# Convolution taps weighed on ScalarE and added in pairs on VectorE, with a higher background rate, in a two-layer conditioned trunk

## The chip, the core and the metric

The kernel runs on one core of a Trainium2 chip. The metric is the device time in microseconds (us) of one execution. TensorE (PE) multiplies matrices, with its weight loads shown as PEld; VectorE (DVE), ScalarE (ACT) and GpSimd (POOL) do the elementwise work; SyncE (SP) issues the DMA transfers of the weights. Each engine works through its own list of instructions in a fixed order, and engines wait for each other through semaphores.

## The reference

Two layers over 256 tokens of 2048 channels, in float32. The first layer mixes tokens with a 31-tap depthwise causal convolution on 1024 channels beside a gated chunk mixer on the other 1024; the second with causal pooling. Each layer then has a dense SwiGLU. Every sub-layer is scaled, shifted and gated by vectors that are computed from a conditioning vector `c`.

```python
def reference(x, c, ...):
    cond = silu(c)
    for l in range(2):
        sh1, sc1, g1, sh2, sc2, g2 = split(cond @ ada_w[l] + ada_b[l], 6)
        h = rmsnorm(x, norm_mix_g[l]) * (1 + sc1) + sh1
        y = mixer_ab(h, ...) if l == 0 else mixer_c(h, ...)
        x = x + g1 * y
        h = rmsnorm(x, norm_ffn_g[l]) * (1 + sc2) + sh2
        x = x + g2 * ((silu(h @ ffn_w1[l]) * (h @ ffn_w3[l])) @ ffn_w2[l])
    return rmsnorm(x, final_g)

def mixer_ab(h, ...):
    a_val, a_gate, b_u, b_v = split(h @ w_in, 4)          # 1024 columns each
    a = a_val * sigmoid(a_gate)
    a = causal_depthwise_conv(a, conv_w) + conv_b          # 31 taps per channel
    a = silu(layernorm(a, a_g, a_b))
    b = b_u * chunk_mix(layernorm(b_v))
    return concat(a, b) @ w_out
```

## The kernel before

**Splits and units.** Every weight comes from memory as a `raw` tile of 128x1024 float32 (12 buffers), on SP's queue. `split` turns it into two parts of a lower precision: `hi` by a cast on ACT (L164), and `lo`, the rest, by a subtraction on DVE (L165); there are four buffers of each. PE multiplies the activations with them (L213 and L214 with `hi`, L219 with `lo`): twelve matmuls of 128x512 for one split. A `unit` is two splits, 24 matmuls. `chain` runs the units of one result, and the 128x512 results lie in PSUM tiles called `mm`.

**Work beside the units.** Two mechanisms put other work between the units.

- `tick`, called after every unit, adds `rate` to a credit and runs one step of the background list `bg` for each whole credit. In the first mixer (`mixer_ab`) the list holds 56 steps: the gate `g1` (16 steps, sums on PE at L312), four quarters of the second scale `SC2` (5 steps each, on PE at L378, then a column step at L405 to L415) and four quarters of the second shift `SH2` (5 steps each). A quarter of the shift is summed on DVE: each of its first four steps has four instructions on `accq` (L383, L385, 128x512) and two weight loads, and its fifth turns the sum into columns on PE (`ps_col`, L405) and adds the bias (L411). `RATES[0]` is the rate of this stage, which has 36 units. What is left in the list by its end is run in `started`, at the beginning of the first SwiGLU: there `between` runs the steps of a quarter beside the units of the quarter ahead of it, and `close` finishes it.
- `split` calls `filler` `FILL` times, and each call runs the generators in `fill` up to their next `yield`. There are three: `conv(0)`, `conv(4)` and `norm_a`.

**The convolution.** `aT` holds the gated values with channels on partitions, eight tiles of 128 channels, and `co` the running sum. `conv` goes through the 31 taps for two channel tiles at a time: L670 for the first tap, with the bias, then L675, which multiplies a shifted window of `aT` by one weight per partition and adds it to `co`, 128x256, on DVE. There is a `yield` after each of the 248 instructions. `norm_a` is the layer norm over channels that follows: column sums on PE (`ps_ln`, L685), mean on ACT, subtraction on DVE (L690), squares on ACT (`sq`), sums on PE (`ps_var`, L698), a power on POOL, a copy on DVE (`rw`), a transposed spread on PE (`ps_rstd`, L711), a product on DVE (L713), SiLU on ACT (L716), and the split into `mh` (ACT, L488) and `ml` (DVE, L489), which are the left operands of the last matmuls.

**Order in the mixer.** The fillers start after the first unit of `proj(DH + 512)`. Then come the other three units of it, eight units for `v`, eight for `u` and eight for `out_half(1)`, the half of the output projection that takes the gated chunk mixer: 27 units. Whatever is then left in `fill` is run at once, and `out_half(0)`, eight units, multiplies the convolution's result. After every two units of an output half, `residual` multiplies by the gate (`gy`, L598) and adds to `x` (L599) on DVE, for both blocks of 128 tokens. At the end, `x` is normalized (`xr`, L476), transposed, scaled and split for the first SwiGLU.

The order on each engine is settled before the run by the framework in which the kernel is written, from the order of the calls and from priorities (`soon` raises one); it can differ from the order of the code.

Of the kernel before, what the change touches and what calls it, by code (L numbers as in the profile page):

```python
# [8 lines left out]
F32 = mybir.dt.float32  # L9
F32R = mybir.dt.float32r  # L10
AF = mybir.ActivationFunctionType
ALU = mybir.AluOpType
PSUM = bass.MemoryType.PSUM

P = 128
D = 2048
KT = D // P
T = 256
# [6 lines left out]
PADC = 16  # L25
EPS = 1e-6
RAW, HL = 12, 4
RATES = 1.28, 0.71, 0.5, 1.0, 1.0
PE2 = False
PE3 = True  # L30
FILL = 5
SOON = 100
WINDOWS = (2, 4, 8, 16)
SH1, SC1, G1, SH2, SC2, G2 = range(6)
# [2 lines left out]
class Trunk:  # L37
# [122 lines left out]
    def split(self, raw):  # L160
# [4 lines left out]
        nc.vector.tensor_tensor(lo, raw, hi.bitcast(F32), op=ALU.subtract)  # L165
        for _ in range(FILL):
            self.filler()
# [436 lines left out]
    def mixer_ab(self, e, nxt):  # L604
        nc, i = self.nc, self.i
        with ExitStack() as s:
            p = s.enter_context(self.tc.tile_pool(name="ab", bufs=1))
            aT = p.tile([P, HT, PADA + T], F32, name="aT")
            nc.gpsimd.memset(aT[:, :, :PADA], 0.0)
            wcT = p.tile([P, HT, P], F32, name="wcT")  # L610
            cw = p.tile([P, HT, 32], F32, name="cw")
# [33 lines left out]
            for b in range(NB):  # L645
                e.start(b)
                for q in range(4):
                    e.prep(b, q)
            held = self.started(e, [(w_in, 0), (w_in, DH), (w_in, 512)], RATES[0], params)
            act = e.act  # L650

            co = p.tile([P, HT, T], F32, name="co", tag="co")
# [9 lines left out]
            done = []  # L662

            def conv(k0):
                for t0 in (k0, k0 + 2):
                    for j in range(CW):
                        for k in (t0, t0 + 1):
                            src = aT[:, k, j : j + T]
                            if j == 0:
                                nc.vector.tensor_scalar(  # L670
                                    co[:, k, :], src, cw[:, k, 0:1], self.col("conv_b", k),
                                    op0=ALU.mult, op1=ALU.add,
                                )
                            else:
                                nc.vector.scalar_tensor_tensor(  # L675
                                    co[:, k, :], src, cw[:, k, j : j + 1], co[:, k, :],
                                    op0=ALU.mult, op1=ALU.add,
                                )
                            yield

            def norm_a():
# [61 lines left out]

            gated(0, held[0], held[1])
            self.late.append(lambda: self.fill.append(conv(0)))
            gated(1, held[2], proj(DH + 512))
            self.late.append(lambda: self.fill.extend([conv(4), norm_a()]))


# [126 lines left out]
    def ffn(self, p, l, e, nxt, gen_g2, rest):  # L876
# [6 lines left out]
        if e.parts:  # L883
            for q in range(1, 4):
                e.prep(0, q)
            for q in range(4):
                e.prep(1, q)
            ps = self.started(e, [(w1, 0), (w3, 0), (w1, 512)], RATES[1])
            held = {(1, 0): ps[0], (3, 0): ps[1], (1, 1): ps[2]}
        else:  # L890
            ps = self.begun(e, [(w1, 0), (w3, 0), (w1, 512)], rest)
            self.rate = RATES[2]
            held = {(1, 0): ps[0], (3, 0): ps[1], (1, 1): ps[2]}
# [72 lines left out]
    def run(self):  # L966
# [32 lines left out]
        with ExitStack() as s:  # L999
# [9 lines left out]
            self.finish(more)  # L1009
            self.rate = RATES[3]  # L1010
            rest = self.add(
                self.mod_cols(1, SC2, 3, PE3, ffn1.gs, "ffn_g"), self.mod_cols(1, SH2, 3, PE3, ffn1.sh)
            )
            self.mixer_c(mix1, ffn1)
            self.rate = RATES[4]
            self.g2 = self.gate()
# [59 lines left out]
```

## Time and profile before

| | |
|---|---|
| median of 3 runs | 2015.34 us (2014.14 to 2020.6) |
| profiled execution, its time | 2013.25 us |
| its span, first to last instruction | 2011.5 us |
| mean clock granted to TensorE | 0.98 |
| first mixer after its first four results begin (started) | about 165 to 429 us |
| change-over to the first SwiGLU | 429 to 443 us |
| start of the first SwiGLU (`started`) | 443 to about 515 us |

Times in the profile are counted from the first instruction. In a row of the timeline the first two numbers are start and duration in us, `xN` means that N instructions were merged in the row, and the bracket gives how long the engine was idle before it and what it waited for. Instructions of one engine overlap a little, so that the distance between two starts is shorter than a duration; sums go by the distance.

### The profile page before, as it was taken

Reading aid. Unit: us, or ns where it says so; the run is one execution under the profiler, and the core shown is the slowest. Engines: PE = TensorE matmul, PEld = TensorE weight load, DVE = VectorE, ACT = ScalarE, POOL = GpSimd, SP = SyncE. Lnnn points to the kernel's source line nnn. Section 1 sums busy time; section 2 is a strip of 40 time slices with the busy share of each in tenths; the row PEclk is TensorE's granted clock in tenths of the full one; section 3 lists DMA queues with packets and bytes.
Section 4 is the critical chain, followed back from the end, with each engine's and each line's share of the span. In section 5 each row is a group of like instructions: output and inputs, shape, how many; then the busy total and the mean of one; then the engine's idle time right before and its main releaser. Section 6 shows DMA issues by size and latency. Waiting matters only on the chain.

```text
span 2011.5 us, 24248 instructions
## 1 busy us (share of the span) xinstructions
PE 1947.4 (97%) x8864; PEld 1541.1 (77%) x8864; DVE 1431.0 (71%) x1724; ACT 839.6 (42%) x1021; POOL 34.7 (2%) x91
## 2 busy tenths in 40 slices
PE   4989999998999999999999999999999999999998
PEld 2557677777887888887878887888788888888886
DVE  4767999798878878777887788867555444554455
ACT  3234343454444344443344346544434444334443
POOL 1000000000000000000120000000000000000000
PEclk7889999989999999999999999999999999999999
DMA  8997988789888899988988887989666666566651
GB/s 337 347 366 258 341 275 291 271 264 350 301 278 321 320 337 328 311 288 317 335 316 296 283 288 263 338 272 319 198 188 189 190 192 191 180 191 193 191 186 46
DMA packets 250344, 540.39 MB, mean 269 GB/s; under 512 B 16521, under 2 KB 17849, under 8 KB 249840
## 3 DMA queue, kind: packets, MB, share of 16 engines
q1 hardware_dynamic: 248472, 536.99, 78.4%
q10 hardware_dynamic: 1752, 1.86, 0.3%
q8 instruction: 69, 1.13, 0.2%
q14 instruction: 51, 0.42, 0.1%
HBM read 536.68 MB, written 2.10 MB: 268 GB/s over the span
## 4 chain that ended last, share of the span: by engine, by line
PE 94%; DVE 2%; DMA 2%; ACT 1%; issue 1%; POOL 0%; SPq 0%; POOLq 0%; DVEq 0%; ACTq 0%
PE mm L213 28%; PE mm L214 27%; PE mm L219 27%; PE ps_ada L378 2%; PE ps_col L405 2%; DVE accq L385 1%; PE mt L213 1%; PE mt L214 1%; PE mt L219 1%; PE tp L590 1%; PE ps_ada L312 1%; PE tp L479 1%; DMA prm<-in_a_conv_w_dram 1%; PE tp L837 1%; DMA raw<-in_pool_w_dram 0%
## 5 line engine op out<-in xcount | busy, mean ns | idle before, releaser
L164 ACT CAST hi<-raw 128x1024 fp32r<-128x1024 f32 x632 | 665.3, 1054 | 974.2 <-PE mm L214 898.8
L165 DVE TENSOR_TENSOR lo<-raw,hi 128x1024 fp32r<-128x1024 f32 x632 | 770.6, 1223 | 419.1 <-ACT hi L164 410.4
L213 PE MATMUL mm<-hi,ah 128*128 128x512 f32 x1568 | 618.4, 395 | 2.9 <-ACT ah L488 2.9
L214 PE MATMUL mm<-hi,al 128*128 128x512 f32 x1568 | 612.2, 391 | 0.0
L219 PE MATMUL mm<-lo,ah 128*128 128x512 f32 x1568 | 421.9, 390 | 0.0
L213 PEld LDWEIGHTS mm<-hi,ah 128*128 128x128 f32 x1568 | 295.6, 189 | 91.8 <-issue 14.3
L214 PEld LDWEIGHTS mm<-hi,al 128*128 128x128 f32 x1568 | 295.5, 188 | 61.5 <-issue 0.8
L219 PEld LDWEIGHTS mm<-lo,ah 128*128 128x128 f32 x1568 | 294.4, 188 | 61.2
L213 PE MATMUL mm<-hi,hh 128*128 128x512 f32 x704 | 280.4, 398 | 0.0
L214 PE MATMUL mm<-hi,hl 128*128 128x512 f32 x704 | 277.3, 394 | 0.0
L350 DVE SCALAR_TENSOR_TENSOR acc<-raw,cond,acc 128x1024 f32<-128x1024 f32 x180 | 230.5, 1280 | 5.4 <-DMA raw<-in_ada_w_dram 3.7
L219 PE MATMUL mm<-lo,hh 128*128 128x512 f32 x704 | 194.7, 395 | 0.0
L213 PEld LDWEIGHTS mm<-hi,hh 128*128 128x128 f32 x704 | 132.3, 188 | 34.9 <-ACT hi L164 1.7
L219 PEld LDWEIGHTS mm<-lo,hh 128*128 128x128 f32 x704 | 132.2, 188 | 31.9
L214 PEld LDWEIGHTS mm<-hi,hl 128*128 128x128 f32 x704 | 132.3, 188 | 30.4
L385 DVE SCALAR_TENSOR_TENSOR accq<-raw,cond,accq 128x512 f32<-128x512 f32 x150 | 112.3, 749 | 2.9 <-DMA raw<-in_ada_w_dram 0.2
L675 DVE SCALAR_TENSOR_TENSOR co<-aT,cw,co 128x256 f32<-128x256 f32 x240 | 99.5, 476 | 0.0
L213 PE MATMUL mm<-hi,mh 128*128 128x512 f32 x160 | 64.1, 402 | 1.6 <-ACT mh L488 1.6
L598 DVE TENSOR_TENSOR gy<-mm,gate 128x512 f32<-128x512 f32 x72 | 47.0, 685 | 24.2 <-PE mm L219 23.9
L214 PE MATMUL mm<-hi,ml 128*128 128x512 f32 x160 | 62.9, 395 | 0.3 <-DVE ml L489 0.3
L378 PE MATMUL ps_ada<-raw,cond 128*32 128x512 f32 x320 | 53.7, 653 | 0.0
L599 DVE TENSOR_TENSOR x<-x,gy 128x512 f32<-128x512 f32 x72 | 47.1, 686 | 0.1
(167 smaller groups left out, 993.8 us busy)
## 6 DMA issues: line engine op xcount, KB each, us to landing
raw<-in_ffn_w_dram SPq DMA_DIRECT2D x528, 512.0 KB
raw<-in_ada_w_dram SPq DMA_DIRECT2D x384, 512.0 KB
raw<-in_ab_w_in_dram SPq DMA_DIRECT2D x64, 512.0 KB
raw<-in_ab_w_out_dram SPq DMA_DIRECT2D x32, 512.0 KB
raw<-in_pool_w_dram SPq DMA_DIRECT2D x8, 512.0 KB
x<-in_x_dram SPq DMA_DIRECT2D x2, 1024.0 KB
gate<-in_final_g_dram SPq DMA_DIRECT2D x1, 1024.0 KB
out_dram<-x SPq DMA_DIRECT2D x2, 512.0 KB
```

The lines of the kernel that those rows point to most:

```text
L164: nc.scalar.copy(hi, raw)
L165: nc.vector.tensor_tensor(lo, raw, hi.bitcast(F32), op=ALU.subtract)
L213: nc.tensor.matmul(ps[b], act[b][0][:, kk, :], hi[:, k, :], start=first and kk == 0, stop=False)
L214: nc.tensor.matmul(ps[b], act[b][1][:, kk, :], hi[:, k, :], start=False, stop=False)
L219: self.nc.tensor.matmul(ps[b], act[b][0][:, kk, :], lo[:, k, :], start=False, stop=last and kk == 3)
L350: nc.vector.scalar_tensor_tensor(acc, raw, self.cond[:, k : k + 1], acc, op0=ALU.mult, op1=ALU.add)
L378: nc.tensor.matmul(acc[32 * j : 32 * j + 32, :], self.cond[:, k : k + 1].to_broadcast([P, 32]), raws[j // 2][:, j % 2, :], start=u == 0, s ...
L385: nc.vector.scalar_tensor_tensor(acc, raws[j // 2][:, j % 2, :], self.cond[:, k : k + 1], acc, op0=ALU.mult, op1=ALU.add)
L405: nc.tensor.matmul(ps[:, a : a + 1], src[:, P * a : P * a + P], one, start=u == 0, stop=u == len(parts) - 1,)
L598: nc.vector.tensor_tensor(t, ps, g[:, 512 * q : 512 * q + 512], op=ALU.mult)
L599: nc.vector.tensor_tensor(xs, xs, t, op=ALU.add)
L675: nc.vector.scalar_tensor_tensor(co[:, k, :], src, cw[:, k, j : j + 1], co[:, k, :], op0=ALU.mult, op1=ALU.add,)
```

## The change

In `conv`, the multiplication of a tap moves to ACT: for each of two channel tiles an ACTIVATE multiplies a window of `aT` by its weight (L676 with the bias for the first tap, straight into `co`; L680 for the others, into a `tap` tile of 128x2x256). One addition on DVE, 128x512, then adds both halves to `co` (L683). The tap tiles alternate between the buffers `s1` and `hm`, two of each, which the stage also uses for `sg`, `at` and `bo`. There are 248 ACTIVATEs and 120 additions where there were 248 instructions on DVE, and 368 places to yield where there were 248. `FILL` goes from 5 to 7, that is from 10 to 14 fillers in a unit. `RATES[0]` goes from 1.28 to 1.56, so that 55 of the 56 background steps run within the mixer's 36 units, where 45 did: the last column step of the shift alone is left for the SwiGLU.

```diff
-RATES = 1.28, 0.71, 0.5, 1.0, 1.0
+RATES = 1.56, 0.71, 0.5, 1.0, 1.0
...
-FILL = 5
+FILL = 7
...
             def conv(k0):
                 for t0 in (k0, k0 + 2):
+                    dst = co[:, t0 : t0 + 2, :]
                     for j in range(CW):
-                        for k in (t0, t0 + 1):
-                            src = aT[:, k, j : j + T]
+                        t = dst
+                        if j > 0:
+                            t = self.wk.tile([P, 2, T], F32, name="tap", tag=("s1", "hm")[j % 2])
+                        for a in range(2):
+                            k = t0 + a
+                            src, w = aT[:, k, j : j + T], cw[:, k, j : j + 1]
                             if j == 0:
-                                nc.vector.tensor_scalar(
-                                    co[:, k, :], src, cw[:, k, 0:1], self.col("conv_b", k),
-                                    op0=ALU.mult, op1=ALU.add,
+                                nc.scalar.activation(
+                                    t[:, a, :], src, AF.Identity, scale=w, bias=self.col("conv_b", k)
                                 )
                             else:
-                                nc.vector.scalar_tensor_tensor(
-                                    co[:, k, :], src, cw[:, k, j : j + 1], co[:, k, :],
-                                    op0=ALU.mult, op1=ALU.add,
-                                )
+                                nc.scalar.activation(t[:, a, :], src, AF.Copy, scale=w)
+                            yield
+                        if j > 0:
+                            nc.vector.tensor_tensor(dst, dst, t, op=ALU.add)
                             yield
```

All lines behind `conv` have numbers higher by five in the changed kernel (L690 becomes L695, L711 becomes L716).

On DVE, the end of the convolution before the change, in the third pair of units of `out_half(1)` (`gy<-mm_2700` belongs to that pair):

```order
L165 TENSOR_TENSOR lo<-raw,hi 128x1024
L675 SCALAR_TENSOR_TENSOR co<-aT,cw,co 128x256 x5
L414 TENSOR_TENSOR sc<-ps_col,adab 128x4
L165 TENSOR_TENSOR lo<-raw,hi 128x1024
L415 SCALAR_TENSOR_TENSOR gs_142<-sc,cols 128x4
L675 SCALAR_TENSOR_TENSOR co<-aT,cw,co 128x256 x5
L165 TENSOR_TENSOR lo<-raw,hi 128x1024
L675 SCALAR_TENSOR_TENSOR co<-aT,cw,co 128x256 x3
L165 TENSOR_TENSOR lo<-raw,hi 128x1024
L690 TENSOR_TENSOR co<-co,mean 128x2048
L598 TENSOR_TENSOR gy<-mm_2700,gate 128x512
```

The same end after the change (`mm_3098` belongs to the fourth and last pair of units of `out_half(1)`):

```order
L683 TENSOR_TENSOR co<-co,tap 128x512
L165 TENSOR_TENSOR lo<-raw,hi 128x1024
L683 TENSOR_TENSOR co<-co,tap 128x512
L383 TENSOR_SCALAR accq<-raw,cond 128x512
L683 TENSOR_TENSOR co<-co,tap 128x512
L385 SCALAR_TENSOR_TENSOR accq<-raw,cond,accq 128x512
L165 TENSOR_TENSOR lo<-raw,hi 128x1024
L695 TENSOR_TENSOR co<-co,mean 128x2048
L385 SCALAR_TENSOR_TENSOR accq<-raw,cond,accq 128x512
L165 TENSOR_TENSOR lo<-raw,hi 128x1024
L385 SCALAR_TENSOR_TENSOR accq<-raw,cond,accq 128x512
L598 TENSOR_TENSOR gy<-mm_3098,gate 128x512
```

The last addition and the subtraction of the mean now stand ahead of the fourth pair's product, where they stood ahead of the third's, and sums of the shift (`accq`) stand between them; before, the first of those sums came behind the fourth pair.

On PE, what follows the statistics of `norm_a` before the change (`mm_2828` and `mm_2829` are the results of the fourth pair of units of `out_half(1)`, whose second unit, two splits, begins in these rows):

```order
L378 MATMUL ps_ada<-raw,cond 32x512
L711 MATMUL ps_rstd<-ident,rw 128x128 x2
L378 MATMUL ps_ada<-raw,cond 32x512 x3
L213 MATMUL mm_2828<-hi,mh_2437 128x512
L214 MATMUL mm_2828<-hi,ml_2438 128x512
L213 MATMUL mm_2828<-hi,mh_2437 128x512
L214 MATMUL mm_2828<-hi,ml_2438 128x512
L213 MATMUL mm_2829<-hi,mh_2441 128x512
```

And after the change (`mm_3292` and `mm_3293` are the first results of `out_half(0)`, and `mh_3241` is the convolution's own result):

```order
L703 MATMUL ps_var<-ones,sq 128x1 x2
L219 MATMUL mm_3099<-lo,mh_2655 128x512
L703 MATMUL ps_var<-ones,sq 128x1 x10
L716 MATMUL ps_rstd<-ident,rw 128x128 x2
L213 MATMUL mm_3292<-hi,mh_3241 128x512
L213 MATMUL mm_3293<-hi,mh_3245 128x512
L214 MATMUL mm_3292<-hi,ml_3242 128x512
```

Before, the two splits of that unit and eleven matmuls on `ps_ada` stood between the spread of the reciprocal deviation and the first use of the result; now nothing does.

## The prediction

> **What bounds the kernel now.** I read the engines' shares first, then the stages of the first mixer and of the SwiGLU's start, then the places where PE waits, since a saved microsecond counts only there.
>
> ```profile
> PE 1947.4 (97%) x8864; PEld 1541.1 (77%) x8864; DVE 1431.0 (71%) x1724; ACT 839.6 (42%) x1021; POOL 34.7 (2%) x91
> ```
> ```profile
> core 0: us, PE busy (x) PEld busy (x) DVE busy (x) ACT busy (x) POOL busy (x), PEclk, DMA share, GB/s
> 200.00:260.00 60.00, 60.00 (x303) 39.93 (x302) 56.69 (x109) 19.46 (x24) 2.26 (x2) 1.00 0.94 337
> 300.00:345.00 45.00, 45.00 (x224) 31.74 (x224) 42.11 (x82) 16.68 (x19) 0.00 (x0) 1.00 0.81 279
> 380.00:429.00 49.00, 47.07 (x216) 37.75 (x208) 46.88 (x66) 26.16 (x40) 0.87 (x1) 1.00 0.94 328
> 443.00:484.00 41.00, 40.85 (x184) 33.81 (x185) 36.76 (x51) 20.13 (x27) 0.00 (x0) 1.00 0.85 292
> 484.00:500.00 16.00, 10.53 (x49) 8.57 (x47) 14.23 (x22) 5.86 (x8) 0.00 (x0) 0.92 1.02 387
> 500.00:504.00 4.00, 3.73 (x8) 2.65 (x9) 2.42 (x4) 1.24 (x3) 0.00 (x0) 0.50 0.94 332
> ```
>
> PE bounds the mixer: it is busy without a gap from 200 to 260 and from 300 to 345 us. DVE, however, is busy 94% there, and 96% from 380 to 429 us: taking work off DVE in the convolution buys nothing by itself, but adding to it near the end costs at once. PE does lose time at 484 to 504 us, and there the shift is to blame:
>
> ```profile
> 378.86 1.92 PE L378 MATMUL ps_ada<-raw,cond 128*32 128x512 f32 x16
> 382.34 1.02 PE L213 MATMUL mm<-hi,mh 128*128 128x512 f32 x2 [1.56 <-ACT mh L488]
> 385.14 1.07 PE L219 MATMUL mm<-lo,mh 128*128 128x512 f32 x4
> 387.86 1.07 PE L219 MATMUL mm<-lo,mh 128*128 128x512 f32 x4
> 388.77 0.95 PE L405 MATMUL ps_col<-pick,rows 128*128 128x1 f32 x8
> 496.81 1.32 PE L405 MATMUL ps_col<-ones,accq 128*128 128x1 f32 x8 [3.60 <-DVE accq L385]
> 500.27 2.27 PE L213 MATMUL mm<-hi,ah 128*128 128x512 f32 x4 [2.15 <-ACT ah L488]
> ```
>
> At 496.81 PE waits 3.60 us for the last quarter's sum and then 2.15 us for what is made from it, and the clock granted afterwards is 0.50. The same rows give PE's prices: a split of twelve matmuls takes 2.72 us (385.14 to 387.86), sixteen `ps_ada` instructions 1.92 us (two for each one listed in the order), a column step 0.8 us. In the mixer, PE waits only 1.56 us for the convolution's result, at 382.34.
>
> **The gain (E).** Nothing of the sums is left at 484 us. The waits of 3.60 and 2.15 us go, and with them the slow clock, from 500.27 to 504 us at least, half of it lost: 2.0 us. E = -7.8 us.
>
> **The prices of what moves.**
>
> ```profile
> L165 DVE TENSOR_TENSOR lo<-raw,hi 128x1024 fp32r<-128x1024 f32 x632 | 770.6, 1223 | 419.1 <-ACT hi L164 410.4 <-DMA raw<-in_ada_w_dram 3.0 <-PE mm L219 2.4
> L385 DVE SCALAR_TENSOR_TENSOR accq<-raw,cond,accq 128x512 f32<-128x512 f32 x150 | 112.3, 749 | 2.9 <-DMA raw<-in_ada_w_dram 0.2
> L675 DVE SCALAR_TENSOR_TENSOR co<-aT,cw,co 128x256 f32<-128x256 f32 x240 | 99.5, 476 | 0.0
> L599 DVE TENSOR_TENSOR x<-x,gy 128x512 f32<-128x512 f32 x72 | 47.1, 686 | 0.1
> L845 ACT ACTIVATE h<-tp,gs 128x128 f32<-128x128 f32 x16 | 5.0, 385 | 2.3 <-PE tp L837 2.3
> L716 ACT ACTIVATE co<-co,cols 128x256 f32<-128x256 f32 x8 | 4.0, 587 | 0.0
> ```
> ```profile
> 326.50 1.29 DVE L598 TENSOR_TENSOR gy<-mm,gate 128x512 f32<-128x512 f32 x2 [1.10 <-PE mm L219]
> 327.70 1.28 DVE L599 TENSOR_TENSOR x<-x,gy 128x512 f32<-128x512 f32 x2
> 332.42 1.22 DVE L165 TENSOR_TENSOR lo<-raw,hi 128x1024 fp32r<-128x1024 f32 x1
> 333.55 2.07 DVE L675 SCALAR_TENSOR_TENSOR co<-aT,cw,co 128x256 f32<-128x256 f32 x5
> 335.53 1.22 DVE L165 TENSOR_TENSOR lo<-raw,hi 128x1024 fp32r<-128x1024 f32 x1
> 403.19 0.74 DVE L385 SCALAR_TENSOR_TENSOR accq<-raw,cond,accq 128x512 f32<-128x512 f32 x1
> 403.85 1.22 DVE L165 TENSOR_TENSOR lo<-raw,hi 128x1024 fp32r<-128x1024 f32 x1
> 426.19 2.00 ACT L164 CAST hi<-raw 128x1024 fp32r<-128x1024 f32 x2
> ```
>
> From start to start, DVE pays 1.13 us for `lo`, 0.40 for an old tap (1.98 / 5), 0.66 for a sum of the shift, and 0.60 for an addition of 128x512 in SBUF (`x<-x,gy`), which is the form of the new one. Over the stage the exchange looks good: 248 x 0.40 = 99 us go, 120 x 0.60 = 72 come, and the 32 sums that move in add 21. DVE ends with 6 us less. What matters is where the work stands.
>
> **A, ScalarE in the convolution.** A tap has one operand per partition and 256 elements. Below it lies L845 (one such operand, half the size, 5.0 / 16 = 0.31 us), above it L716 (two, same size, 4.0 / 8 = 0.50). I take 0.40, in the middle. The densest stretch in the new order lies between the copies of `v`'s first half and the transposes of the first `bo`: 99 taps, 4 first taps at 0.50, 22 casts `hi` at 0.95 (two in 2.00 us, of 1.05 each), and some 10 us of other work, together 72 us; on PE 18 splits (49.0 us), 52 listed `ps_ada` (12.5) and some 8 of other work, together 70. ACT comes out 2 us late, which four `hi` buffers, 11 us of PE's work, can cover; but taps, additions and casts now wait for each other in both directions. A = +2 us, from 0 to +12 (at 0.50 a tap, ACT is 12 us late there). [...]
>
> **B, the last taps on VectorE.** Before, 248 fillers of the convolution at 10 a unit were through after 24.8 of the 27 units; now 368 at 14 take 26.3, and the shift's sums begin after 36 / 1.56 = 23 units, where they began after 28. So they meet. DVE cannot do the second `gy` of the first pair of `out_half(1)` before PE has finished that pair; from there to the last addition its list holds 12 `lo` (13.6 us), 23 additions (13.8), 15 sums (9.9) and 2 first ones at 0.40 (0.8), 11 `gy` and `x` (6.6), 0.3 of columns: 45.0 us. In the same stretch PE has ten splits (27.2), 8 `ps_ada` (1.9) and two column steps (1.6): 30.7 us, and then `ps_ln` needs that last addition. B = +14.3 us. This is a floor as far as DVE's prices hold, since its list admits no overtaking; if an addition waits for its taps it grows, by up to 6.
>
> **C, the norm without cover.**
>
> ```profile
> 364.11 2.29 PE L698 MATMUL ps_var<-ones,sq 128*128 128x1 f32 x20
> 366.44 0.16 DVE L704 TENSOR_SCALAR rv<-ps_var 128x2 f32<-128x2 f32 x1 [3.51 <-PE ps_var L698]
> 368.32 0.29 DVE L708 COPY rw<-rv 128x256 f32<-128x256 f32 x1 [0.59 <-POOL rv L705]
> 372.27 2.29 DVE L713 TENSOR_TENSOR co<-co,ps_rstd 128x2048 f32<-128x2048 f32 x1 [1.39 <-PE ps_rstd L711]
> 359.43 2.19 ACT L693 ACTIVATE sq<-co 128x512 f32<-128x512 f32 x4 [0.54 <-DVE co L690]
> 377.74 4.04 ACT L716 ACTIVATE co<-co,cols 128x256 f32<-128x256 f32 x8
> 381.69 2.16 ACT L488 CAST mh<-co 128x512 fp32r<-128x512 f32 x4
> 431.29 0.68 DVE L599 TENSOR_TENSOR x<-x,gy 128x512 f32<-128x512 f32 x1
> ```
>
> From the last addition: a sum and a `lo` stand ahead of the subtraction (1.8 us), the subtraction itself (2.3, as L713), squares (2.2), the last `ps_var` (2.3), `rv` to `rw` (1.9), a sum, `rw` and the spread (1.7), the product (2.3), SiLU (4.0), the first `mh` (0.6): 19.1 us. The first `ml` comes later still: behind the product stand five sums, three `x` and `gy` and a `lo`, 6.3 us, so that PE goes on at about 21. Of PE's work there are left two splits (5.4) and its own parts of the chain (about 5): PE idles some 10.5 us, where the row at 382.34 shows 1.56 and little more behind it. With 1 us for a slow clock behind the idle time (the 0.50 above), C = +9.5, from +4 to +13.
>
> **D and F, the end of the mixer and the change-over.** In `out_half(0)` DVE carries about the same as before (56 us of list from the product to the last `x`, against 57.4 us measured, from 372.27 + 2.29 to 431.29 + 0.68), so PE ends no earlier relative to the product: D = +1.5. In the change-over, ten sums stand among the `xr` where six stood: 4 x 0.66, F = +2.5, from 0 to +4. The other moved steps cost PE nothing: the same matmuls, earlier. Their 16 loads (8.4 MB) move from 484 us, where the DMA is full, to the mixer's last units, which now last longer; while `g1` is summed 337 GB/s at a share of 0.94 leave a rate that is 22% higher little room, and the 12 `raw` buffers cover that for some units. I put it at nothing, and at 5 us if the cover is gone; that is in A's end.
>
> **Sum.** 2.0 + 14.3 + 9.5 + 1.5 + 2.5 - 7.8 = +22.0 us, on 2013.25 us for the profiled execution 2035.3. The median of the runs shown is 2.1 us above that execution, so I forecast 2037 us.
>
> **The rivals.**
>
> *Faster: the lag is covered.* The wait at 496 us goes and nothing takes its place: 2015.3 - 7.8 = 2007.5 us. That needs B to vanish. Its point is the price of an addition: at or below 14.3 / 23 = 0.62 us less than I take, that is for nothing, DVE would keep up. L599, 0.60 us for the same form over 72 instances, speaks against it. Chance 0.07.
>
> *No change: half of it.* Were PE behind already when the stretch of B begins, or the norm's chain shortened because its first rows overlap more, 8 us of losses would cancel the gain: 2015 us. The lists speak against it. Chance 0.05.
>
> *ScalarE becomes the bound.* At 0.50 us a tap, or with casts that queue behind taps that wait for a buffer, ACT leads the whole convolution: 248 x 0.1 = 25 us more ACT work, of which the 12 us of the densest stretch reach PE, with up to 6 in B: 2037 + 10 to 16, about 2050 us. For it speaks that ACT goes from 19.5 of 60 us to about 52 (some 80 taps more); against it that PE's units are longest there. Chance 0.16.
>
> *The rate doesn't do what it says.* If steps were left over, the wait at 496 us would stay. The list of PE shows one column step behind the transposes and no more; I give it nothing.
>
> **How the numbers follow.** The forecast, with 2026 to 2046 us as its own range, has 0.72. The range takes in the ScalarE case and part of the weaker losses: 2018 to 2051 us leaves out the faster and the equal case (0.12) and a tail above (0.07). A measurement of this kernel tells 0.3% (6 us) from no change; by the cases, faster 0.08, within it 0.05, slower 0.87.
>
> **What would show it.** In the profile after: no wait of PE for `accq` near the SwiGLU's start (E); DVE without idle time from the first `gy` of `out_half(1)` to the subtraction of the mean, and PE waiting there for `lo` or for `co`, 14 us or more (B); an idle PE of about 10 us ahead of the first matmul on the convolution's `mh` (C); a tap of 0.4 us from start to start and PE without long waits before (A). I am wrong if PE reaches `ps_ln` without having waited, or if an addition costs much less than `x<-x,gy`.

## The result, and the profile after

The changed kernel takes 2033.65 us (2032.9 to 2034.87, four runs) beside 2016.74 us (2014.14 to 2020.6, four runs) for the kernel before: a ratio of 1.0085, interval 1.0068 to 1.0101. It is slower by some 17 us. Each run below stands beside executions of the kernel before from its own batch, whose medians lie between 2013.96 and 2016.74 us. The profiled execution took 2033.72 us, 20.5 more than the 2013.25 of the one before, and that is the difference taken apart below.

The page's first part after the change, and the two new groups of the convolution:

```profile
PE 1951.4 (96%) x8864; PEld 1544.3 (76%) x8864; DVE 1412.2 (69%) x1596; ACT 936.3 (46%) x1269; POOL 34.2 (2%) x91
```
```profile
L680 ACT ACTIVATE tap<-aT,cw 128x256 f32<-128x256 f32 x240 | 102.4, 501 | 26.1 <-DVE co L683 14.4 <-PE tp L590 7.8 <-PE tp L744 3.9
L683 DVE TENSOR_TENSOR co<-co,tap 128x512 f32<-128x512 f32 x120 | 82.6, 689 | 18.9 <-ACT tap L680 13.1
```

DVE works 19 us less than before, ACT 97 us more, and the kernel is slower: the totals don't tell why. The stages do (busy time of each engine by stretch, after the change):

```profile
core 0: us, PE busy (x) PEld busy (x) DVE busy (x) ACT busy (x) POOL busy (x), PEclk, DMA share, GB/s
200.00:260.00 60.00, 59.16 (x297) 38.13 (x296) 50.19 (x67) 55.35 (x116) 0.53 (x1) 1.00 0.93 339
336.30:384.40 48.10, 39.38 (x160) 28.89 (x159) 46.16 (x69) 30.99 (x58) 0.00 (x0) 0.89 0.79 260
380.00:429.00 49.00, 39.12 (x175) 32.21 (x174) 40.24 (x52) 20.75 (x32) 1.15 (x1) 0.81 0.65 211
484.00:515.00 31.00, 31.00 (x139) 25.66 (x138) 17.96 (x19) 14.25 (x17) 0.00 (x0) 1.00 0.70 211
```

In the convolution PE is nearly full and ACT now stands at 55 of 60 us. From 336 to 384 us DVE is nearly full (46.16 of 48.10 us) and PE is not; from 380 to 429 PE had 47.07 us with the clock at 1.00 before, and has 39.12 at 0.81 now. The start of the SwiGLU, from 484 us, is without a gap. The same stretch before the change:

```profile
484.00:515.00 31.00, 25.25 (x105) 20.30 (x104) 24.77 (x32) 12.30 (x16) 0.00 (x0) 0.89 0.87 314
```

PE's long waits after the change, in the timeline (rows between them left out):

```profile
355.31 1.20 PE L219 MATMUL mm<-lo,mh 128*128 128x512 f32 x4 [1.35 <-DVE lo L165]
...
363.84 1.20 PE L219 MATMUL mm<-lo,mh 128*128 128x512 f32 x4 [2.80 <-DVE lo L165]
...
375.78 1.83 PE L405 MATMUL ps_col<-ones,accq 128*128 128x1 f32 x8 [4.57 <-DVE accq L385]
...
383.32 2.75 PE L690 MATMUL ps_ln<-co,ones 128*128 128x256 f32 x12
...
397.99 1.19 PE L716 MATMUL ps_rstd<-ident,rw 128*128 128x128 f32 x4 [1.90 <-DVE rw L713]
406.21 1.31 PE L213 MATMUL mm<-hi,mh 128*128 128x512 f32 x2 [7.03 <-ACT mh L488]
408.48 0.79 PE L214 MATMUL mm<-hi,ml 128*128 128x512 f32 x1 [0.95 <-DVE ml L489]
...
460.05 0.76 PE L479 MATMUL tp<-ident,xr 128*128 128x128 f32 x4 [4.28 <-DVE xr L476]
462.97 5.08 PE L479 MATMUL tp<-ident,xr 128*128 128x128 f32 x20 [2.16 <-DVE xr L476]
```

First PE waits for DVE's list (three waits, 8.7 us, up to 375.78), then for the norm, whose result it needs at 406.21 with nothing left to do, then for `xr`. Before, the place at `mh` cost it 1.56 us, and the one at `xr`:

```profile
430.17 0.66 PE L479 MATMUL tp<-ident,xr 128*128 128x128 f32 x4 [1.25 <-DVE xr L476]
433.08 1.11 PE L479 MATMUL tp<-ident,xr 128*128 128x128 f32 x4 [2.26 <-DVE xr L476]
```

DVE's own list after the change, from the second `gy` of the first pair of `out_half(1)` to the subtraction of the mean:

```profile
336.27 1.29 DVE L598 TENSOR_TENSOR gy<-mm,gate 128x512 f32<-128x512 f32 x2
...
383.69 0.68 DVE L683 TENSOR_TENSOR co<-co,tap 128x512 f32<-128x512 f32 x1
...
387.62 2.29 DVE L695 TENSOR_TENSOR co<-co,mean 128x2048 f32<-128x2048 f32 x1 [1.45 <-ACT mean L692]
...
399.29 2.29 DVE L718 TENSOR_TENSOR co<-co,ps_rstd 128x2048 f32<-128x2048 f32 x1 [0.78 <-PE ps_rstd L716]
```

To see where time goes between kernels whose waits differ, I counted PE's lost time from split to split: the time from the first matmul of one split to that of a later one, less 2.72 us for each split between and less PE's other matmuls at fixed prices (0.12 us for each `ps_ada` instruction of the trace, 0.10 for a one-column matmul on `ps_col`, 0.11 to 0.25 for the others; in the trace before, sixteen `ps_ada` take 1.85 us, eight on `ps_col` 0.81, sixteen transposes 1.70 to 1.80, one matmul on `ps_bc` 0.23 to 0.31). It contains idle time, slow clock and small delays alike. Splits are numbered from the kernel's first; the counting begins with number 24, at about 165 us. The last unit of `out_half(1)` begins at split 78, and the change-over follows split 95. A few microseconds of the norm's own work on PE are in it for every kernel, and in the change-over the 32 transposes of `xr`, for which nothing is taken off; interleaved `ps_ada` can cost more than the fixed price (how much is told with the light sums below), so differences are read, not the entries themselves.

| lost by PE, us | up to split 68 (A) | 68 to 81 (B and C) | 81 to 95 (D) | change-over, 95 to 100 (F) | SwiGLU's start, 100 to 118 (E) | sum |
|---|---|---|---|---|---|---|
| before | 7.9 | 8.8 | 0.3 | 13.5 | 8.7 | 39.2 |
| after | 10.5 | 30.7 | 0.4 | 17.9 | 0.0 | 59.5 |
| after less before | +2.6 | +21.9 | +0.1 | +4.4 | -8.7 | +20.3 |

### The profile page after: what moved, and what is told of

Same layout as the page of the kernel before. It is cut to its first block, busy times and chain, and to the rows that moved or that the text cites. A ratio compares the mean times of both kernels' runs of the same rounds, so it can differ in the third digit from the quotient of the medians.

```text
span 2032.0 us, 24438 instructions
## 1 busy us (share of the span) xinstructions
PE 1951.4 (96%) x8864; PEld 1544.3 (76%) x8864; DVE 1412.2 (69%) x1596; ACT 936.3 (46%) x1269; POOL 34.2 (2%) x91
## 3 DMA queue, kind: packets, MB, share of 16 engines
q10 hardware_dynamic: 1752, 1.86, 0.3%
## 4 chain that ended last, share of the span: by engine, by line
PE 92%; DVE 4%; DMA 2%; issue 1%; ACT 1%; POOL 0%; SPq 0%; POOLq 0%; DVEq 0%; ACTq 0%
PE mm L213 27%; PE mm L214 27%; PE mm L219 27%; PE ps_ada L378 2%; DVE accq L385 2%; PE ps_col L405 1%; PE mt L213 1%; PE mt L214 1%; PE mt L219 1%; PE tp L590 1%; PE ps_ada L312 1%; DVE lo L165 1%; DMA prm<-in_a_conv_w_dram 1%; DMA raw<-in_ada_w_dram 1%; PE tp L842 1%
## 5 line engine op out<-in xcount | busy, mean ns | idle before, releaser
L350 DVE SCALAR_TENSOR_TENSOR acc<-raw,cond,acc 128x1024 f32<-128x1024 f32 x180 | 230.5, 1281 | 17.7 <-DMA raw<-in_ada_w_dram 16.3
L680 ACT ACTIVATE tap<-aT,cw 128x256 f32<-128x256 f32 x240 | 102.4, 501 | 26.1 <-DVE co L683 14.4
L683 DVE TENSOR_TENSOR co<-co,tap 128x512 f32<-128x512 f32 x120 | 82.6, 689 | 18.9 <-ACT tap L680 13.1
L598 DVE TENSOR_TENSOR gy<-mm,gate 128x512 f32<-128x512 f32 x72 | 47.5, 686 | 24.5 <-PE mm L219 24.2
```

The lines of the kernel that those rows point to most:

```text
L350: nc.vector.scalar_tensor_tensor(acc, raw, self.cond[:, k : k + 1], acc, op0=ALU.mult, op1=ALU.add)
L598: nc.vector.tensor_tensor(t, ps, g[:, 512 * q : 512 * q + 512], op=ALU.mult)
L680: nc.scalar.activation(t[:, a, :], src, AF.Copy, scale=w)
L683: nc.vector.tensor_tensor(dst, dst, t, op=ALU.add)
```

## The experiments

The theory: the gain at the SwiGLU's start is real, and is paid several times over because the shift's sums now stand in DVE's list together with the last taps (B), and because the fillers end one unit before the norm's result is needed, so that the chain of the norm is bare (C). The rivals: ScalarE is the bound; or the sums do no harm by themselves and only the new convolution does.

**The rate back to 1.28, the new convolution kept.**

```diff
-RATES = 1.56, 0.71, 0.5, 1.0, 1.0
+RATES = 1.28, 0.71, 0.5, 1.0, 1.0
```

> The changed kernel with RATES[0] back at 1.28, so that the sums of the shift come after the convolution again. My theory (the place of the work on DVE): the list from the second gate product of the first pair of out_half(1) to the last addition falls from 45.0 to 35.9 us beside 34.9 of PE, so the lag B goes almost whole (16.6 us of PE lost between split 68 and 78 in the changed kernel); the norm still has no cover (C stays at about 10 us), and the wait for the last quarter of the shift at the SwiGLU's start, 8.7 us, is back. Net 2030 us, from 2026 to 2034. Rival (the ScalarE taps and their coupling with DVE are what costs, not the sums): B stays, the gain goes: 2042 us.

2029.53 us (2028.09 to 2030.3) beside 2015.56, ratio 1.0058 (1.0038 to 1.0079): as forecast. From split 68 to 78 PE loses 2.6 us, where the changed kernel loses 16.6, so B comes with the higher rate, which brings the sums there. The norm is still bare, though (PE's rows, and one of DVE's):

```profile
380.03 1.19 PE L716 MATMUL ps_rstd<-ident,rw 128*128 128x128 f32 x4 [1.89 <-DVE rw L713]
383.77 1.84 PE L405 MATMUL ps_col<-pick,rows 128*128 128x1 f32 x8 [2.54 <-DVE co L718]
388.25 0.80 PE L213 MATMUL mm<-hi,mh 128*128 128x512 f32 x1 [2.65 <-ACT mh L488]
391.85 0.79 PE L214 MATMUL mm<-hi,ml 128*128 128x512 f32 x1 [2.80 <-DVE ml L489]
```
```profile
386.51 4.69 DVE L385 SCALAR_TENSOR_TENSOR accq<-raw,cond,accq 128x512 f32<-128x512 f32 x6
```

The fillers run 14 a unit at either rate and end at the same unit. From split 78 to 81 PE loses 17.1 us, and the wait of 3.60 us for the last sum is back at 508.83. While PE waits for `ml`, DVE is at six sums of the shift in a row, so the bare chain also has sums in it.

**The higher rate alone, with the old convolution.**

```diff
-RATES = 1.28, 0.71, 0.5, 1.0, 1.0
+RATES = 1.56, 0.71, 0.5, 1.0, 1.0
```

> The kernel before with RATES[0] at 1.56 alone; convolution and FILL as before. My theory: the last tap now has 25.2 us of DVE beside 26.4 of PE, so no lag ahead of the norm, whose cover stays; DVE has about 103 us of list beside 99 of PE from the first pair of out_half(1) to the end of the mixer, so some 5 us are lost there, 4 in the change-over to the SwiGLU, and 8.7 are gained at its start: 2017 us, from 2012 to 2023. Rival (the sums of the shift do not fit into the mixer, whatever the convolution does): the 10 to 15 us of lag stay, 2025 to 2030 us.

2022.78 us (2020.33 to 2026.47), ratio 1.0030 (1.0018 to 1.0042): between the forecast of the theory and that of the rival. (Its profiled execution, from which the table is made, was the slowest of its runs, 2026.47.) So the rate by itself costs 7 us by the medians, although it removes 8.7 at the SwiGLU's start. The loss is not in one place: 4.0 us more than before up to split 68, 3.3 up to 81, 6.3 in `out_half(0)`, 6.0 in the change-over, where PE waits 5.33 us:

```profile
427.27 1.21 PE L219 MATMUL mm<-lo,mh 128*128 128x512 f32 x4 [2.00 <-DVE lo L165]
452.82 1.12 PE L479 MATMUL tp<-ident,xr 128*128 128x128 f32 x4 [5.33 <-DVE xr L476]
```

I had given `out_half(0)` too much room: the changed kernel loses nothing there, and I take that to be because PE had already been held up ahead of it, which no run shows by itself.

**More fillers a unit, at the new rate: `FILL` 8 and 9.**

```diff
-FILL = 7
+FILL = 8
```

> The changed kernel with FILL 8 in place of 7: 16 fillers a unit, so that the convolution ends after 23 units. My theory: only 12 additions and 4 sums are left behind the first pair of out_half(1), 16.7 us of DVE beside 15.4 of PE; B falls to 2 us or less and the norm has six splits or more of cover (C about 1); ScalarE is denser, A rises from 2.7 to about 5: 2021 us, from 2016 to 2027. Rival (ScalarE is the bound, or it is the amount of work and not its place): 2034 us or slower.

2026.79 us (2023.5 to 2027.63), ratio 1.0043 (1.0027 to 1.0058): within the range, 6 us above the forecast. The norm's wait is gone (0.4 us from split 78 to 81), B is not: 13.3 us from 68 to 78, where I had forecast 2 or less. The additions are through earlier, and sums of the shift stand ahead of the `lo` for which PE waits; how much of the loss their time makes is tested below. Then 8.9 us are lost in `out_half(0)`.

```profile
381.69 1.88 PE L219 MATMUL mm<-lo,mh 128*128 128x512 f32 x4 [4.10 <-DVE lo L165]
437.20 1.22 PE L219 MATMUL mm<-lo,mh 128*128 128x512 f32 x2 [2.78 <-DVE lo L165]
453.29 0.83 PE L479 MATMUL tp<-ident,xr 128*128 128x128 f32 x4 [4.04 <-DVE xr L476]
```

> The changed kernel with FILL 9: the convolution ends ahead of the first gate product of out_half(1). My theory: B and C as with FILL 8 or a little less, but ScalarE now has about 8.0 us of work a unit (12 taps of 0.427, two casts, copies) beside some 7.2 on PE, over 20 units, of which four hi buffers cover 11: A rises to about 10 us. 2024 us, from 2019 to 2031. Rival (earlier is better, ScalarE hidden): 2017 us or faster than FILL 8. Rival (amount of work): 2034 us or slower.

2029.65 us (2027.79 to 2030.47), ratio 1.0063 (1.0042 to 1.0084): within the range, 6 us above the forecast. The norm is covered too, but the loss ahead of split 68 rises from 11.2 to 20.1 us. From 260 to 330 us, with `FILL` 8 and 9:

```profile
260.00:330.00 70.00, 69.70 (x375) 49.01 (x373) 59.14 (x82) 59.53 (x128) 1.92 (x2) 1.00 0.85 302
```
```profile
260.00:330.00 70.00, 69.16 (x351) 45.84 (x349) 62.39 (x89) 64.43 (x142) 1.99 (x2) 1.00 0.83 288
```

ACT goes from 59.53 to 64.43 of 70 us, and PE gets through 351 matmul records instead of 375. ACT is not full, however, and PE is idle for no more than 1.1 us up to split 68. That ScalarE is the limit is therefore not shown. Most of the loss has another place, told with the light sums below: the same 248 `ps_ada` instructions take PE 40.2 us instead of 33.5.

**Both numbers: rate 1.28 and `FILL` 8.**

```diff
-RATES = 1.56, 0.71, 0.5, 1.0, 1.0
+RATES = 1.28, 0.71, 0.5, 1.0, 1.0
...
-FILL = 7
+FILL = 8
```

> The changed convolution with RATES[0] back at 1.28 and FILL 8: the sums of the shift stay out of the convolution, which ends after 23 units and leaves the norm with cover. My theory (the moved convolution costs only through the norm that lost its cover, 17 us between split 78 and 81 with FILL 7 at this rate): that falls to 3 us or less, the losses before split 68 rise by 1 to 3 us (ScalarE denser), the rest is as in the kernel before: 2017 us, from 2013 to 2021. Rival (ScalarE's taps and the additions cost by themselves, wherever the norm stands): 2025 us or slower.

2007.84 us (2005.39 to 2009.25) beside 2013.96, ratio 0.9968 (0.9957 to 0.9980): 9 us better than forecast, and faster than before. One filler more in a split takes 22 us off the kernel with the rate back. Up to split 81 PE loses 9.6 us, where the kernel before loses 16.7: with their end early enough, the new convolution is a gain. Whether that is DVE's relief or the earlier end alone is not separated, since the old convolution with more fillers was not run.

**The other half of the change, without the mixer.** In the kernel before, what is left of the third and fourth quarters is run one quarter earlier within the SwiGLU's start; nothing moves into the mixer.

```diff
-        ffn0.parts = list(zip(scale, shift))
+        z = list(zip(scale, shift))
+        ffn0.parts = [z[0], z[1] + z[2], z[3], ()]
```

> The kernel before with nothing moved into the mixer, but with the last two quarters of the shift summed one quarter earlier inside the start of the SwiGLU: ffn0.parts = [z[0], z[1] + z[2], z[3], ()]. The order has the last sum four splits earlier on DVE and its column step 15 rows earlier on PE. My theory (the 8.7 us at the SwiGLU's start are lost only because 16 sums and the preparation of a quarter, some 20 us of DVE, are due within 16 us of PE): most of the wait goes without any cost in the mixer: 2009 us, from 2005 to 2013. Rival (DVE is full there too, the wait moves to the quarter before): 2015 us, no change.

2007.22 us (2006.45 to 2007.49), ratio 0.9965 (0.9953 to 0.9978): as forecast. The loss from split 100 to 118 falls from 8.7 to 0.6 us, and every other entry of the table stays. E could be had without its price.

**Half of the sums moved.** The same edit with the rate at 1.42 instead of 1.28, old convolution.

```diff
-RATES = 1.28, 0.71, 0.5, 1.0, 1.0
+RATES = 1.42, 0.71, 0.5, 1.0, 1.0
...
+        z = list(zip(scale, shift))
+        ffn0.parts = [z[0], z[1] + z[2], z[3], ()]
```

> The convolution of the kernel before, rate 1.42 (50 of 56 background steps in the mixer: the third quarter of the shift is summed there, the fourth is not), and the fourth quarter summed a quarter earlier at the SwiGLU's start. My theory (each sum of the shift that moves into the mixer's last units costs about its 0.66 us of DVE, since DVE is full there): 16 of the 32 sums that rate 1.56 moved come, half of what they cost (22.8 - 15.6 + 8.7 = 16 us, so 8), against a gain of 8.7 at the start: 2015 us, from 2010 to 2020. Rival (only the last quarter's sums collide, the third fits): 2008 us.

2014.22 us (2011.78 to 2016.09), ratio 0.9997 (0.9988 to 1.0007): as forecast. Against the last run, the five steps moved into the mixer cost 7.0 us in all: 5.0 are lost in `out_half(0)` and 3.9 in the change-over, while 2.6 are saved from split 68 to 81.

**The three that help together: new convolution, rate 1.28, `FILL` 8, quarters earlier.**

> Both edits together: the changed convolution with FILL 8 and rate 1.28, and the last two quarters of the shift summed a quarter earlier. My theory: the effects add up, FILL 8 at this rate +1 to +3 and the earlier sums -6: 2011 us, from 2006 to 2016. Rival (the wait only moves): 2017 us.

2000.47 us (1999.48 to 2002.55) beside 2013.96, ratio 0.9934 (0.9921 to 0.9948): it beats both kernels. The savings of two runs above, 6.1 (both numbers) and 6.7 us (the other half), add up: it saves 13.5. The forecast of 2011 was too high by about as much as the one for `FILL` 8 at the rate of 1.28, which it builds on. The stretch in which the changed kernel fails, and the SwiGLU's start:

```profile
336.30:384.40 48.10, 48.10 (x251) 35.19 (x250) 38.37 (x50) 26.15 (x40) 1.07 (x1) 0.96 0.82 283
484.00:515.00 31.00, 31.00 (x142) 25.39 (x141) 26.75 (x29) 17.10 (x23) 0.00 (x0) 1.00 0.96 345
```

PE is full in both, with DVE at 38 of 48 us instead of 46. And the norm's chain has PE's work beside it:

```profile
348.42 2.29 DVE L695 TENSOR_TENSOR co<-co,mean 128x2048 f32<-128x2048 f32 x1
...
362.17 2.29 DVE L718 TENSOR_TENSOR co<-co,ps_rstd 128x2048 f32<-128x2048 f32 x1 [0.85 <-PE ps_rstd L716]
```

From the subtraction of the mean to the product it takes 13.8 us here, 11.7 in the changed kernel (387.62 to 399.29): the chain is no shorter, it is covered.

**`FILL` 9 on that version.**

> The fastest kernel so far (changed convolution, rate 1.28, shift summed a quarter earlier at the SwiGLU's start) with FILL 9 in place of 8. Theory (ScalarE becomes the bound beyond 16 fillers a unit: 12 taps of 0.427, casts and copies make 8.0 us a unit beside 7): the losses before split 68 rise by about 8 us, as from FILL 8 to 9 at rate 1.56, and nothing is gained behind it: 2008 us, from 2004 to 2012. Rival (a still earlier norm leaves DVE more room, ScalarE is hidden): 2000 us or faster.

2018.38 us (2008.74 to 2020.42, wider than the others) beside 2014.12, ratio 1.0006 (0.9992 to 1.0021). The direction is that of the theory, the size twice what I forecast: the loss ahead of split 68 goes from 4.1 to 21.6 us in the profiled execution, the slowest of its runs. So one filler more than 8 costs about as much as one less; that this is ScalarE's limit is not shown, since ACT is less busy from 200 to 260 us than with `FILL` 8 (55.09 and 57.42 us, rows in the last section). Up to split 68 PE is idle for 3.9 us, is slow behind the first of two waits (sixteen transposes take 3.55 us from 268.67, another sixteen 1.70 from 274.70; the clock is 0.95 from 260 to 330 us), and spends 32.9 us on 200 `ps_ada` instructions that took 25.1 with `FILL` 8.

**The sums made light, at rate 1.56 and `FILL` 8.** Of the shift's sums all but the first of a quarter work on 64 of 512 columns, so that most of the sum is left out; steps, loads and order stay.

```diff
+                    n = 64 if l == 0 and v == SH2 else 512
                     nc.vector.scalar_tensor_tensor(
-                        acc, raws[j // 2][:, j % 2, :], self.cond[:, k : k + 1], acc, op0=ALU.mult, op1=ALU.add
+                        acc[:, :n], raws[j // 2][:, j % 2, :n], self.cond[:, k : k + 1], acc[:, :n],
+                        op0=ALU.mult, op1=ALU.add,
```

> The changed kernel with FILL 8 (rate 1.56), where each later sum of the second shift of the first layer takes 64 columns in place of 512: the loads, the steps and the waits stay, the instruction on DVE shrinks from 0.66 to about 0.15 us, and most of the sum is left out. My theory (what the higher rate costs in the mixer is the time of the moved sums on DVE): the losses behind split 64 fall to those of FILL 8 at rate 1.28 and the wait at the SwiGLU's start stays away: 2007.8 - 8.7 + 3 = 2002 us, from 1998 to 2007. Rival (the loads of the shift, or the steps that crowd PE and the one buffer of the sums, are what costs): 2018 us or slower, near the 2026.8 of FILL 8.

2011.40 us (2009.99 to 2014.2) beside 2014.12, ratio 0.9982 (0.9970 to 0.9993): between the two. A sum of 64 columns is busy for 0.27 us at the least, one of 512 for 0.75; the 0.15 us was my estimate. Of the run at `FILL` 8 15.4 us go with DVE's time for the sums. They go where the theory puts them: 9.0 us in the change-over, 5.1 in `out_half(0)`, 2.0 from split 68 to 81. But 9 us above the forecast remain. From split 68 to 81 PE still loses 11.7 us, where the new convolution with `FILL` 8 loses 5.5 at rate 1.28. So at `FILL` 8 the sums' time on DVE makes only a small part of the loss in that place. PE idles there for 3.0 us, mostly in two waits, and the clock is 0.91 on the mean from 336.3 to 384.4 us: matmuls on `mm` start 0.43 us apart from 368.59 to 371.15 and from 383.14 to 385.27, and 0.23 apart from 373.17 to 374.99. The waits:

```profile
380.11 1.02 PE L407 MATMUL ps_col<-ones,accq 128*128 128x1 f32 x8 [1.34 <-DVE accq L386]
382.41 0.50 PE L213 MATMUL mm<-hi,mh 128*128 128x512 f32 x1 [1.27 <-ACT hi L164]
```

Another 7 us lie ahead of split 68, where the entry is the same as with full sums (11.2 us, and 4.1 at rate 1.28). That is the higher rate itself, not the sums: `g1` and the scale follow each other more closely. The traces show most of what it costs. From its first start to the next matmul, an uninterrupted run of `ps_ada` on PE takes 0.97 to 1.00 us whether it has two, four, six or eight instructions, and, but for one of 2.06, 1.83 to 1.90 with ten to sixteen, where PE does not wait beside it and is not at the slow clock. A step of eight that PE does in two pieces therefore costs twice as much. Two and eight, from the traces of `FILL` 9 and `FILL` 8 at rate 1.28 with the quarters earlier:

```profile
246.31 1.04 PE L312 MATMUL ps_ada<-raw,cond 128*32 128x512 f32 x2
247.28 0.50 PE L213 MATMUL mm<-hi,ah 128*128 128x512 f32 x1
```
```profile
256.40 1.06 PE L312 MATMUL ps_ada<-raw,cond 128*32 128x512 f32 x8
257.39 0.50 PE L213 MATMUL mm<-hi,ah 128*128 128x512 f32 x1
```

Up to split 68, with light sums, PE has 24 runs with 248 instructions in 33.5 us without waits, at rate 1.28 21 runs with 200 in 25.1; 2.6 us of the 8.4 between them are more than the fixed price takes off. Together with 1.6 us of idle time, where the other has none, that is 4.2 of the 7 us; for the rest I found no wait.

The whole table, worked out as above:

| lost by PE, us | to 68 | 68 to 81 | 81 to 95 | 95 to 100 | 100 to 118 | median, us |
|---|---|---|---|---|---|---|
| new convolution, rate 1.28, `FILL` 7 | 5.8 | 19.7 | 0.2 | 16.3 | 10.1 | 2029.53 |
| old convolution, rate 1.56, `FILL` 5 | 11.9 | 12.1 | 6.6 | 19.5 | 0.0 | 2022.78 |
| new, 1.56, `FILL` 8 | 11.2 | 13.7 | 8.9 | 19.0 | 0.0 | 2026.79 |
| the same, light sums | 11.2 | 11.7 | 3.8 | 10.0 | 0.0 | 2011.40 |
| new, 1.56, `FILL` 9 | 20.1 | 5.5 | 8.0 | 19.5 | 0.0 | 2029.65 |
| new, 1.28, `FILL` 8 | 4.1 | 5.5 | 0.3 | 13.9 | 8.7 | 2007.84 |
| old, 1.28, `FILL` 5, quarters earlier | 7.9 | 8.7 | 0.3 | 13.5 | 0.6 | 2007.22 |
| old, 1.42, `FILL` 5, quarters earlier | 9.0 | 6.1 | 5.3 | 17.4 | 0.2 | 2014.22 |
| new, 1.28, `FILL` 8, quarters earlier | 4.1 | 5.5 | 0.3 | 13.9 | 0.7 | 2000.47 |
| new, 1.28, `FILL` 9, quarters earlier | 21.6 | 6.9 | 0.3 | 14.1 | 0.5 | 2018.38 |

## Why the prediction was right

The forecast was +22.0 us on the profiled execution and 2037 us for the median; it came to +20.5 and 2033.65. Step by step:

- **A, +2.0; measured +2.6, but for another reason.** Thirteen taps in a row take 5.21 us from the first start to the cast behind them, 0.40 each, as I had taken from two neighbouring rows; over all 240, single ones among them, it is 102.4 / 240 = 0.427 us of busy time. The addition has the 0.69 us and the spacing of 0.60 that I took (from 232.99 to the next instruction at 233.59). The late taps were not what cost the time, however: with the same taps at rate 1.28 PE loses 5.8 us up to split 68, less than the 7.9 of the kernel before, and with the old taps at rate 1.56 it loses 11.9. The term belongs to the rate, for which I had put down nothing ("The other moved steps cost PE nothing"). Of the 2.6 us, 1.0 is idle time and 0.8 are the shorter runs of `ps_ada` described above (25 with 248 instructions, 33.6 us; before 23 with 200, 27.0 us).

```profile
225.36 5.31 ACT L680 ACTIVATE tap<-aT,cw 128x256 f32<-128x256 f32 x13
230.57 1.03 ACT L164 CAST hi<-raw 128x1024 fp32r<-128x1024 f32 x1
```

- **B, +14.3: the size of the place is right, the difference is too large.** DVE's list took from 336.27 to 384.37, 48.1 us, where I had counted 45.0. It holds the 12 `lo`, 23 additions, 15 sums and two first ones that I had counted; the difference is in the start (47.5 us from the second `gy`), in 1.8 us for which DVE was idle itself (rows below), and in small delays. PE idled 8.7 us there in three waits, where I had named 14 us or more as the sign, and worked at half the clock twice, 3.5 us at 0.51 and 6.0 at 0.50, another 4.7: 13.4. But the kernel before loses time there as well, 1.7 us of it in a stretch at a clock of 0.54 behind no wait at all. So from split 68 to 78 the loss grows by 10.6 us, from 6.0 to 16.6. That these sums' own time makes B at `FILL` 7 rests on DVE's list and on the run with the rate back; a run with light sums was made at `FILL` 8 alone, where it took 2.0 us off. The rows after, and those before:

```profile
350.78 0.69 DVE L598 TENSOR_TENSOR gy<-mm,gate 128x512 f32<-128x512 f32 x1 [1.22 <-PE mm L219]
352.02 0.16 DVE L414 TENSOR_TENSOR sc<-ps_col,adab 128x4 f32<-128x4 f32 x1 [0.55 <-PE ps_col L405]
```
```profile
364.80:368.30 3.50, 3.50 (x11) 2.67 (x10) 3.50 (x6) 3.50 (x7) 0.00 (x0) 0.51 0.96 353
376.00:382.00 6.00, 6.00 (x19) 5.03 (x20) 5.97 (x9) 2.65 (x5) 0.00 (x0) 0.50 0.83 283
```

```profile
336.30:384.40 48.10, 46.26 (x227) 31.86 (x226) 38.02 (x59) 20.57 (x30) 1.61 (x1) 0.96 0.80 268
367.40:371.00 3.60, 3.60 (x10) 1.77 (x8) 2.89 (x4) 1.05 (x1) 0.89 (x1) 0.54 0.52 147
```

- **C, +9.5: too small.** I had 10.5 us of idle time; it is 1.90 + 7.03 + 0.95 = 9.9. The chain was longer than the 19.1 us I had added up, 21.8 from the end of the last addition (384.37) to the first `mh` (406.21), and PE had more work beside it than I had counted. What I sized wrongly is the clock behind it: I took 1 us, but PE worked 4.84 us at 0.50 and 2.00 at 0.83, 2.8 us lost. With the 1.56 us of the kernel before taken off, that is 11.1; from split 78 to 81 the loss grows by 11.4. B and C together were forecast at 23.8 and measured 21.9; how these divide can't be told to the microsecond, since the norm's own matmuls lie ahead of split 78 in the kernel before and behind it after.

```profile
406.00:412.00 6.00, 4.84 (x10) 3.38 (x11) 6.00 (x10) 2.28 (x5) 0.00 (x0) 0.50 0.63 214
412.00:414.00 2.00, 2.00 (x9) 1.58 (x8) 1.62 (x3) 0.49 (x1) 0.00 (x0) 0.83 0.90 266
```

- **D, +1.5: measured +0.1.** This says little: in the run at rate 1.56 with the old convolution the same place loses 6.3 us more than before, probably since PE comes to it less late.
- **F, +2.5: measured +4.4.** More sums among the `xr`: PE waits 4.28 us for the first where it waited 1.25 before, the second wait is the same (2.16 and 2.26), and PE waits another 0.86 for the remaining column step's sum.
- **E, -7.8: measured -8.7.** Both waits and the slow clock are gone, as the rows from 484 to 515 us show.

That the total fits within 2 us is partly luck: B and C together came out 1.9 us too large, D 1.4 too large and the gain E 0.9 too small, against 1.9 us too little for F and 0.6 for A, whose cause was another.

Of the rivals, that ScalarE becomes the bound fails at `FILL` 7, where the run with the rate back loses 5.8 us up to split 68; at `FILL` 9 the loss is there, but that ACT causes it is not shown. That the lag would be covered is what happens at rate 1.28 with `FILL` 8: not by a cheaper addition, which I named as the only point, but by an earlier end of the convolution and the sums kept out of the list. The sentence that taking work off DVE in the convolution buys nothing by itself is in doubt: at rate 1.28 and `FILL` 8 it goes with 6 us, but the earlier end came with it, and no run separates the two.

## What to carry to other kernels

Work that fills gaps has a deadline where its result is needed, and a serial chain behind it (here some 22 us of norm) needs its length in other work of the bounding engine after the last filler: count the units left, not the mean load. Before moving work out of a visible wait, look for a place near it where the engine has room, since an edit of two lines within the SwiGLU's start brought 6.7 us, where the move into the full mixer alone cost 7 net. Edits that come together are best priced one by one: each of the two here, put right, is worth 6 to 7 us, and the change, with one filler too few in a split and the steps of the shift in the wrong stage, costs 17. And count in how many pieces small matmuls are put between large ones, since two of them can cost as much as eight (0.97 and 0.99 us here).

## What the runs showed of the hardware

- The granted clock fell where no wait shows. In the kernel before, at 364.11, PE does twenty matmuls of one column in 2.29 us, is busy all the time by its records, and is granted 0.54 from 367.4 to 371 us (row above). The kernels with rate 1.28 and `FILL` 8, with the quarters earlier, and with both are slow behind the same twenty matmuls too, without a wait of PE: eight `ps_ada` take 1.86 us from 359.78 in the first, two take 1.52 from 370.13 in the second, eight take 1.86 from 358.88 in the third, where the clock is 0.61 from 358.5 to 362 us; elsewhere in these traces two take 0.97 to 0.98 and eight 0.99 to 1.00. After the change, a wait of 2.80 us (363.84) is followed by 3.50 us at 0.51 (row above), so that it cost 1.7 us more than its length.

  Why the clock falls there, no run here shows.
- A PE that is busy for all of a stretch need not do the same work in it: from 200 to 260 us PE has 60.00 us busy in both of these kernels, with 311 matmul records at `FILL` 8 and 283 at `FILL` 9 (rate 1.28, quarters earlier). On `mm` it is 199 and 187, in transposes 24 and 8, and the 88 on `ps_ada` are busy for 11.30 us in one and 15.24 in the other (the last two rows, of `ps_ada` alone). The loss of 17.5 us up to split 68 is only partly in the idle time of 3.9.

```profile
200.00:260.00 60.00, 60.00 (x311) 40.61 (x309) 53.49 (x73) 57.42 (x121) 2.46 (x2) 1.00 0.94 340
```
```profile
200.00:260.00 60.00, 60.00 (x283) 37.25 (x282) 48.68 (x64) 55.09 (x118) 0.00 (x0) 1.00 0.93 341
```
```profile
200.00:260.00 60.00, 11.30 (x88) 1.92 (x88) 0.00 (x0) 0.00 (x0) 1.00 0.94 340
```
```profile
200.00:260.00 60.00, 15.24 (x88) 2.52 (x88) 0.69 (x1) 0.00 (x0) 1.00 0.93 341
```

- A short run of `ps_ada` (32 columns of weights) between other matmuls takes PE 0.97 us with two instructions and 0.99 with eight (rows above, with the light sums).
